# Moving four tile pools by 64 or 96 bytes in a float32 diffusion-transformer kernel

## The chip, the cores and the metric

The kernel runs on one core of one Trainium2 chip. The metric is the device time of one execution in microseconds (us), a median over runs. TensorE multiplies, with a stationary operand that is loaded first (a weight load, PEld in the profile) and a streamed operand that passes through it (the matmul, PE). VectorE (DVE), ScalarE (ACT) and GpSimd (POOL) do the elementwise work, SyncE (SP) starts most of the transfers.

## What is computed

Two layers of a diffusion transformer over 512 latent tokens and, in the first layer, 256 context tokens, model width 1024, all in float32. Both layers scale and shift their input with values made from a conditioning vector, and both end in a gated feed-forward block. Layer 0 mixes tokens by grouped attention (16 heads, 4 key heads, width 64, rotary embedding), layer 1 by a gated linear recurrence in two directions (8 heads of 128):

```python
for i in range(DEPTH):
    hn_l = modulate(rms_norm(h, norm_mix_w[i]), sh1_l, sc1_l)
    hn_c = modulate(rms_norm(hc, norm_mix_w[i]), sh1_c, sc1_c)
    y_l, y_c = attention_mixer(...) if i == 0 else hgrn2_mixer(...)
    h = h + gt1_l * y_l
    h = h + gt2_l * swiglu(modulate(rms_norm(h, norm_ffn_w[i]), sh2_l, sc2_l), ffn_w_in[i], ffn_w_out[i])
    if not last: hc = ...            # the same for the context
return rms_norm(h, final_norm_w)
```

## The kernel before

**Stages, in order of time.** To about 430 us: conditioning values, keys and values, queries, attention and its output projection. 430 to 940 us: the feed-forward block of layer 0 over 768 tokens, in two column blocks of 384. 940 to 1420 us: the recurrence, head by head. From 1420 us: the feed-forward block of layer 1 over 512 tokens, in two column blocks of 256, and the output.

**Products.** A product in float32 is made of two parts, high and low, of each operand, and of three matmuls (`mm3`, lines 116 to 120: high times high, high times low, low times high). Each matmul has a 128x128 stationary operand, which is loaded anew for every matmul, and streams 256, 384 or 512 columns. In both feed-forward blocks, the weights of a hidden tile are combined so that seven products of 12 matmuls do the work of eight (`pair_units`, line 1213; `m1` to `m7`, lines 1082 to 1130): they stream the operands `xb11`, `xb21`, `xt1`, `xt2`, `xt4`, `xb22` and `xt3` in this order (in layer 1, `xb11` and `xb21` lie in a tile called `xw`). The first hidden tiles are made plainly (`plain`, line 1039, tile `ffi`). The second half of the block streams the hidden values `gh` and `gl` and keeps the output weights stationary (`fo_mm`, line 1133, tile `ffo`). In the recurrence, `hz` and `hq` (`trans_proj`, line 1626) stream the normalised input `hn` over stationary weights, and `hv` and `hg` (`token_proj`, line 1615) stream the weights over stationary `hn`. In attention, `po` (line 798) streams the probabilities `pth` and `ptl` over the stationary values `vv`. The scan itself (`lv`, line 1725) streams `QD` over the stationary `kc`. `wo` and `hwo` stream attention's and the recurrence's result (`o`, `oth`) over stationary output weights.

**Where tiles lie.** A tile takes the same bytes in each of 128 partitions. The program rounds a tile up to 32 bytes and puts it behind the one before; pools are stacked from the low end, or from the high end (`side="right"`; within such a pool the first tile is still the lowest). So the byte address of each operand follows from the sizes. Weights on their way to TensorE lie in `ring`, whose tiles all start at a multiple of 128. The other operands start, modulo 128, at:

| operand (pool) | streamed or stationary | start mod 128 |
|---|---|---|
| `whi`, `wlo` (`ring`) | stationary, in `hv` and `hg` streamed | 0 |
| `hnh`, `hnl` of layer 0 (`hn0p`) | stationary | 96 |
| `pth`, `ptl` (`att`); `vv` | streamed; stationary | 0; 0 |
| `o` (`o4p`), `oth`, `otl` (`hgrno`) | streamed | 96 |
| `xb11`, `xb21`, `xt4`, `xb22`, `xt2` of layer 0, `hn` of layer 1 (`hnp`) | streamed, in `hv` and `hg` stationary | 0 |
| `xt3`, `xt1` of layer 0 (`ffn0`) | streamed | 0, 64 |
| `gh`, `gl` of layer 0 (`ffn0`, `ffn0g`) | streamed | 32 or 64, by the slot |
| `kc`, `QD` (`hgrn`) | stationary, streamed | 32, 32 |
| `xw`, `xt4`, `xb22`, `xt3` of layer 1 (`ffn1`) | streamed | 0 |
| `xt1`, `xt2` of layer 1 (`ffn1`) | streamed | 32, 64 |
| `gh`, `gl` of layer 1; `foh`, `fol` (`ffn1`) | streamed; stationary | 32 or 64; 64 |

The text calls the difference of the two starts modulo 128 the offset of a matmul. With weights in `ring` it is the start of the other operand. A tile that comes to lie on the bytes of older tiles waits for their last users.

**The three tiny tiles** hold reciprocal root mean squares, six numbers a partition (24 bytes, so 32). `rstd_of` (line 290) makes them; `rc0` and `rc1` are made in the feed-forward blocks (lines 1330, 1343 and 1427), the third in `norm_tail` (line 1565), in the pool `ffn0g`.

Of the kernel before, what the change touches and what calls it, by code (L numbers as in the profile page):

```python
# [8 lines left out]
F32 = mybir.dt.float32  # L9
# [7 lines left out]
P = 128  # L17
D = 1024
KT = D // P
NL = 512  # L20
NC = 256
T = NL + NC
NT = T // P
# [26 lines left out]
def kernel(  # L50
# [13 lines left out]
    def pool(name, es=None, **kw):  # L64
        return (es or ctx).enter_context(tc.tile_pool(name=name, bufs=1, reuse_waits="tile", **kw))
# [16 lines left out]
    def bank(name):  # L82
        return psums["pool"].tile([P, 512], F32, tag="b", bufs=psums["bufs"]["b"], name=name)
# [32 lines left out]
    def mm3(ps, ahi, alo, bhi, blo, first, last, onto=False):  # L116
        kw = dict(skip_group_check=True) if onto else {}
        PE.matmul(ps, ahi, bhi, start=first, stop=False, **kw)  # L118
        PE.matmul(ps, ahi, blo, start=False, stop=False, **kw)  # L119
        PE.matmul(ps, alo, bhi, start=False, stop=last, **kw)  # L120
# [160 lines left out]
    def rstd_cols(pl, acc, n, tag="rc", late=False):  # L281
        nt = n // P
        pc = bank("ssq")
        for t in range(nt):
            m = PE.matmul(pc[:, 2 * t : 2 * t + 2], acc[:, t * P : (t + 1) * P], ones[:, 0:2], start=True, stop=True)
            if late:
                pin(m)
        return rstd_of(pl, pc, nt, tag)

    def rstd_of(pl, pc, nt, tag="rc"):  # L290
        rc = pl.tile([P, NT], F32, tag=tag, name="rc")[:, :nt]
        DVE.tensor_scalar(rc, pc[:, 0 : 2 * nt].rearrange("p (t v) -> p t v", v=2)[:, :, 0], 1.0 / D, EPS,
                          op0=ALU.mult, op1=ALU.add)
        POOL.tensor_tensor(rc, rc, mhalf.to_broadcast([P, nt]), op=ALU.pow)
        return rc

    def rstd_psum(dg, rc, n, late=False):
        nt = n // P
        dg = dg[:, 0:n].rearrange("p (t q) -> p t q", q=P)
        DVE.tensor_tensor(dg, ident.unsqueeze(1).to_broadcast([P, nt, P]), rc.unsqueeze(2).to_broadcast([P, nt, P]),  # L300
                          op=ALU.mult)
        ps = bank("rstd")[:, 0:n]
        for t in range(nt):
            m = PE.matmul(ps[:, t * P : (t + 1) * P], ones, dg[:, t], start=True, stop=True)
            if late:
                pin(m)
        return ps
# [33 lines left out]
    hnp = pool("hn0p", qes, side="right")  # L341
# [399 lines left out]
    qes.close()  # L741

    hpool = pool("hT", side="right")
    hT = [hpool.tile([P, T], F32, name=f"hT{k}") for k in range(KT)]

    def residual_in():
# [12 lines left out]
    def residual(o, ps, layer, ch, v, a, e):  # L759
        DVE.scalar_tensor_tensor(hT[o][:, a:e], ps, mcol(layer, ch, o, v), hT[o][:, a:e], op0=ALU.mult, op1=ALU.add)  # L760

    ap_ = pool("att", att)
    o4es = ExitStack()
    o4p = pool("o4p", o4es, side="right")
    lasts = []
# [104 lines left out]
    acc_n = pool("accn").tile([P, T], F32, name="acc_n")  # L870
# [8 lines left out]
    def xbank(name):  # L879
        return xps["pool"].tile([P, 512], F32, tag="x", bufs=6, name=name)  # L880
# [3 lines left out]
    def wo_last():  # L884
        (ws, prs), = lasts
        for half in HALVES[0]:
            a0, e0 = half[0][1], half[-1][2]
            banks = {}

            def wos(o, i):  # L890
                if o not in banks:
                    banks[o] = xbank("wos")
                osl = slice(o * P, (o + 1) * P)
                mm3(banks[o][:, 0 : e0 - a0], ws[i][0][:, osl], ws[i][1][:, osl],
                    prs[i][0][:, a0:e0], prs[i][1][:, a0:e0], i == 0, i == 1)

            if a0 == 0:
                for o in range(4):
                    wos(o, 0)
            for o in range(KT):  # L900
                if o not in banks:
                    wos(o, 0)
                wos(o, 1)
                ps = banks.pop(o)
                for v, a, e in half:
                    residual(o, ps[:, a - a0 : e - a0], 0, 2, v, a, e)
                yield
        o4es.close()
# [38 lines left out]
    def ffn(layer, only_lat, pre, begin, tail=None):  # L947
# [4 lines left out]
        parts = PARTS[layer]  # L952
        es = ExitStack()
        fp = pool(f"ffn{layer}", es)

        def operand(m, slot=None):
            p_ = fp if layer or m in ("t1", "t3") else hnp
            if layer and m in ("b11", "b21"):
                if not wide_op:
                    wide_op.append(p_.tile([P, 4, 4, H], F32R, tag="xw", name="xw"))  # L960
                i = 2 * (m == "b21")
                return [wide_op[0][:, i], wide_op[0][:, i + 1]]
            return [p_.tile([P, 4, H], F32R, tag=f"x{slot or m}{c}", name=f"x{m}{c}") for c in "hl"]
# [353 lines left out]
        rc, rst = {}, {}  # L1317
# [244 lines left out]
    rst1 = [None, None]  # L1562
    hg = ExitStack()

    def norm_tail(fp, o):
        if o == 2:
            rst1.append(rstd_cols(fp, acc_n[:, :NL], NL))
        elif o == 4:
            rst1[0] = rstd_psum(fp.tile([P, T], F32, tag="g8", bufs=1, name="dg"), rst1.pop(), NL)

    hnp = pool("hnp", hg)
    ffn(0, False, wo_last(), ada_mix, tail=norm_tail)
    xps["es"].close()
    s2es = ctx.enter_context(ExitStack())
# [355 lines left out]
    for _ in sb:  # L1930
        pass
    hg.close()
    ffn(1, True, wlast, None)


# [46 lines left out]
```

## Time and profile before

| | |
|---|---|
| median of 3 runs | 1802.15 us (1801.05 to 1806.98) |
| the profiled execution | 1801.19 us, its span from first to last instruction 1799.4 us |
| busy: PE, PEld, DVE, ACT, POOL | 97%, 89%, 72%, 48%, 35% of the span |
| instructions | 30616, of which 11717 matmuls and as many weight loads |
| mean granted TensorE clock | 0.994 |

The profile gives for each engine the time in which it worked on something; a matmul's time is counted from its first column to its last result, and the next one starts long before that end. How fast TensorE goes is therefore read from the starts of successive matmuls in the timeline, not from the time of one. Groups of instructions are written as line, engine, operation, tile written and tiles read, stationary columns and streamed shape, count, busy us and mean ns of one, and the engine's idle time before them.

### The profile page before, as it was taken

What the parts mean: (1) busy time and instruction counts of PE and PEld (TensorE: products, weight loads), DVE (VectorE), ACT (ScalarE), POOL (GpSimd) and SP (SyncE); (2) the same over time, 40 slices, a digit from 0 to 9 for tenths busy, and PEclk for the clock granted to TensorE, in tenths of its full rate; (3) what the DMA queues carried; (4) which work ended last, traced back from release to release, by engine and by line L of the source; (5) the groups of instructions that cost most, each with busy time, mean ns of one, the idle gap of its engine ahead of it and who ended that gap; (6) DMA issues with size and microseconds to landing.
All of it is one profiled execution on the core that took longest, in us unless ns stands there. A gap on an engine that the chain in (4) does not pass through costs nothing.

```text
span 1799.4 us, 30616 instructions
## 1 busy us (share of the span) xinstructions
PE 1745.2 (97%) x11717; PEld 1601.1 (89%) x11717; DVE 1301.7 (72%) x2281; ACT 871.7 (48%) x1777; POOL 624.2 (35%) x570
## 2 busy tenths in 40 slices
PE   8999999999899999999999999999999899999998
PEld 6788788898899989999998999898898899999997
DVE  4876788888878888888866555655747658786764
ACT  3544777766533524243446433334334545554544
POOL 2454344434113314132303243224425454333420
PEclk9999999999999999999999999999999899999999
DMA  9534400002134242545331212123211124343322
GB/s 334 174 123 131 148 28 25 24 1 77 33 109 123 65 131 86 164 136 158 94 106 46 71 59 78 53 71 94 71 48 47 56 60 115 100 116 99 100 61 83
DMA packets 213457, 166.42 MB, mean 92 GB/s; under 512 B 7952, under 2 KB 190400, under 8 KB 213312
## 3 DMA queue, kind: packets, MB, share of 16 engines
q1 hardware_dynamic: 213024, 163.43, 29.8%
q8 instruction: 92, 1.51, 0.3%
q10 hardware_dynamic: 288, 1.05, 0.1%
q14 instruction: 53, 0.43, 0.1%
HBM read 162.36 MB, written 2.10 MB: 91 GB/s over the span
## 4 chain that ended last, share of the span: by engine, by line
PE 79%; DVE 8%; ACT 4%; issue 4%; POOL 3%; DMA 2%; SPq 0%; POOLq 0%; ACTq 0%; DVEq 0%
PE ffo L120 5%; PE ffo L118 5%; PE ffo L119 5%; PE x L118 4%; PE x L119 4%; PE x L120 4%; PE pt L787 3%; PE y L118 2%; PE lv L1725 2%; PE y L119 2%; PE y L120 2%; PE hz L118 2%; PE hz L119 2%; PE hz L120 2%; PE sc L729 1%
## 5 line engine op out<-in xcount | busy, mean ns | idle before, releaser
L1732 POOL TENSOR_TENSOR KD<-KD,tot 128x384 f32<-128x384 f32 x96 | 102.8, 1094 | 81.7 <-ACT kc L1715 77.9
L777 POOL TENSOR_SCALAR pf<-pf,st 128x768 f32<-128x768 f32 (+1 forms) x96 | 73.7, 769 | 125.7 <-DVE st L776 89.4
L760 DVE SCALAR_TENSOR_TENSOR hT<-ffo,modc,hT 128x512 f32<-128x512 f32 (+1 forms) x122 | 78.6, 648 | 45.0 <-PE ffo L120 45.0
L120 PE MATMUL ffo<-gh,wlo_w 128*128 128x512 f32 (+1 forms) x304 | 102.6, 338 | 0.0
L119 PE MATMUL ffo<-gl,whi_w 128*128 128x512 f32 (+1 forms) x304 | 102.2, 336 | 0.0
L118 PE MATMUL ffo<-gh,whi_w 128*128 128x512 f32 (+1 forms) x304 | 101.7, 337 | 0.0
L95 DVE TENSOR_TENSOR ptl<-pt,pth 128x384 fp32r<-128x384 f32 (+1 forms) x160 | 79.8, 523 | 12.8 <-ACT pth L90 11.6
L242 DVE SCALAR_TENSOR_TENSOR adacc<-adw,csil,adacc 128x512 f32<-128x512 f32 x98 | 83.3, 860 | 7.7 <-DMA adw<-in_ada_w_dram 7.6
L90 ACT CAST pth<-pt 128x384 fp32r<-128x384 f32 (+1 forms) x160 | 69.8, 461 | 34.0 <-PE pt L787 22.1
L775 ACT ACTIVATE pf<-sc,st 128x768 f32<-128x768 f32 (+1 forms) x96 | 73.5, 765 | 19.0 <-DVE st L773 18.0
L1732 DVE TENSOR_TENSOR QD<-QD,tot 128x256 f32<-128x256 f32 x96 | 52.0, 581 | 41.2 <-PE lv L1725 41.1
L773 DVE TENSOR_REDUCE st<-sc 128x1 f32<-128x768 f32 (+1 forms) x96 | 74.1, 773 | 10.2 <-PE sc L730 8.7
L1715 ACT COPY kc<-KD 128x256 f32<-128x256 f32 x112 | 43.3, 413 | 76.3 <-PE lv L1725 44.5
L787 PE MATMUL pt<-ident,pf 128*128 128x128 f32 x448 | 72.1, 275 | 5.2 <-DVE ptl L95 3.8
L118 PE MATMUL ffo<-gh,foh 128*128 128x512 f32 (+1 forms) x186 | 71.4, 384 | 0.0
L120 PE MATMUL ffo<-gh,fol 128*128 128x512 f32 (+1 forms) x186 | 70.8, 381 | 0.2 <-DVE fol L95 0.2
L119 PE MATMUL ffo<-gl,foh 128*128 128x512 f32 (+1 forms) x186 | 70.9, 381 | 0.0
L1791 POOL TENSOR_SCALAR oss<-oss 128x4 f32<-128x4 f32 (+1 forms) x9 | 4.7, 525 | 181.8 <-DVE oss L1790 181.7
L1725 PE MATMUL lv<-QD,kc 128*128 128x128 f32 x448 | 63.4, 286 | 4.5 <-DVE QD L1732 2.4
L1725 PEld LDWEIGHTS lv<-QD,kc 128*128 128x128 f32 x448 | 58.6, 191 | 8.8 <-ACT kc L1715 3.8
L787 PEld LDWEIGHTS pt<-ident,pf 128*128 128x128 f32 x448 | 51.3, 140 | 13.9 <-issue 6.4
L119 PEld LDWEIGHTS ffo<-gl,whi_w 128*128 128x128 f32 x304 | 57.2, 188 | 6.9
(1114 smaller groups left out, 6772.5 us busy)
## 6 DMA issues: line engine op xcount, KB each, us to landing
adw<-in_ada_w_dram SPq DMA_DIRECT2D x40, 512.0 KB, 4.6
adw<-in_ada_w_dram SPq DMA_DIRECT2D x80, 256.0 KB, 2.9
raw_hz<-in_hgrn_w_in_dram SPq DMA_DIRECT2D x14, 512.0 KB, 3.7
adr<-in_ada_w_dram SPq DMA_DIRECT2D x16, 256.0 KB, 5.4
adr<-in_ada_w_dram SPq DMA_DIRECT2D x8, 512.0 KB, 7.9
raw_wq<-in_attn_w_qkv_dram SPq DMA_DIRECT2D x8, 512.0 KB, 5.4
raw_wo<-in_attn_w_o_dram SPq DMA_DIRECT2D x8, 512.0 KB, 3.4
raw_hv<-in_hgrn_w_in_dram SPq DMA_DIRECT2D x8, 512.0 KB, 4.3
```

The source lines that it names most:

```text
L95: m = (eng or DVE).tensor_tensor(lo, src, hi.bitcast(F32), op=ALU.subtract)
L118: PE.matmul(ps, ahi, bhi, start=first, stop=False, **kw)
L119: PE.matmul(ps, ahi, blo, start=False, stop=False, **kw)
L120: PE.matmul(ps, alo, bhi, start=False, stop=last, **kw)
L242: pin(DVE.scalar_tensor_tensor(a, raw, cc, a, op0=ALU.mult, op1=ALU.add))
L760: DVE.scalar_tensor_tensor(hT[o][:, a:e], ps, mcol(layer, ch, o, v), hT[o][:, a:e], op0=ALU.mult, op1=ALU.add)
L773: DVE.tensor_reduce(st3[:, 0:1], ps[:, :nk], op=ALU.max, axis=AX.X, negate=True)
L775: ACT.activation(pf, ps[:, :nk], AF.Exp, bias=st3[:, 0:1], accum_out=st3[:, 1:2])
L777: POOL.tensor_scalar(pf, pf, st3[:, 2:3], 1.0, op0=ALU.mult, op1=ALU.mult)
L787: PE.transpose(pt[:, i * P : (i + 1) * P], pf[:, (i0 + i) * P : (i0 + i + 1) * P], ident)
L1725: PE.matmul(ps[:, cs], kc[:, cs], mv, start=True, stop=True)
L1732: eng.tensor_tensor(view, view, f, op=ALU.mult)
```

## The change

Four pools begin with a tile that nothing uses, and three tiny tiles get longer. No instruction is added or taken away.

```diff
     def rstd_of(pl, pc, nt, tag="rc"):
-        rc = pl.tile([P, NT], F32, tag=tag, name="rc")[:, :nt]
+        rc = pl.tile([P, {"rc0": 32, "rc1": 32, "rct": 16}.get(tag, NT)], F32, tag=tag, name="rc")[:, :nt]
...
     hpool = pool("hT", side="right")
+    hpool.tile([P, 24], F32, name="shift")
...
     ap_ = pool("att", att)
+    ap_.tile([P, 16], F32, name="shift")
...
         fp = pool(f"ffn{layer}", es)
+        if layer:
+            fp.tile([P, 16], F32, name="shift")
...
     def norm_tail(fp, o):
         if o == 2:
-            rst1.append(rstd_cols(fp, acc_n[:, :NL], NL))
+            rst1.append(rstd_cols(fp, acc_n[:, :NL], NL, "rct"))
...
     hnp = pool("hnp", hg)
+    hnp.tile([P, 16], F32, name="shift")
```

By the same rule of sizes, everything in `att` moves up by 64 bytes; everything in `hnp`, and in `hgrn` and `ffn0` which lie on top of it, by 64; everything in `ffn1` by 64; in `ffn0` and `ffn1`, what lies behind `rc0` by 96 more, and behind `rc1` by another 96. On the right side, `hT` stays, and `o4p` and `hgrno` below it move down by 96, `ffn0g` by 96 and 32. The starts become:

| operand | start mod 128 before | after |
|---|---|---|
| `pth`, `ptl` (over `vv` at 0) | 0 | 64 |
| `o`, `oth`, `otl` | 96 | 0 |
| `xb11`, `xb21`, `xt4`, `xb22`, `xt2`, `xt3` of layer 0; `hn` of layer 1 | 0 | 64 |
| `xt1` of layer 0 | 64 | 64 |
| `gh`, `gl` of layer 0 | 32 or 64 | 64 |
| `kc`, `QD` | 32, 32 | 96, 96 |
| `xw`, `xt4`, `xb22`, `xt3`, `xt1`, `xt2` of layer 1 | 0, 0, 0, 0, 32, 64 | 64 |
| `gh`, `gl` of layer 1 over `foh`, `fol` | 32 or 64 over 64 | 64 over 64 |

So matmuls with `ring` weights in the feed-forward blocks, `hz`, `hq`, `hv`, `hg` and `po` come to an offset of 64. `ffo` of layer 1, `wo` and `hwo` come to, or stay at, an offset of 0, and the scan's stay at 0.

## The prediction

> **What bounds the kernel now.** I read the page first, then the busy time by stage, then the timeline of TensorE matmul by matmul, then the groups by shape.
>
> ```profile
> PE 1745.2 (97%) x11717; PEld 1601.1 (89%) x11717; DVE 1301.7 (72%) x2281; ACT 871.7 (48%) x1777; POOL 624.2 (35%) x570
> ...
> PE 79%; DVE 8%; ACT 4%; issue 4%; POOL 3%; DMA 2%; SPq 0%; POOLq 0%; ACTq 0%; DVEq 0%
> ```
>
> TensorE is the bound: busy for 97% of the span, and 79% of the chain that ended last is its matmuls. The other engines can hardly become the bound through this change, which gives them no instruction.
>
> ```profile
> 430.00:940.00 510.00, 503.80 (x2877) 477.15 (x2876) 413.82 (x649) 211.71 (x418) 128.92 (x87) 1.00 0.36 107
> 940.00:1420.00 480.00, 469.88 (x3250) 432.05 (x3249) 295.11 (x491) 201.80 (x364) 166.97 (x154) 1.00 0.21 63
> 1420.00:1799.00 379.00, 364.00 (x2548) 340.38 (x2546) 266.55 (x443) 191.20 (x425) 143.25 (x110) 0.98 0.31 90
> ```
>
> The columns after the stage and its length are busy PE, PEld, DVE, ACT and POOL, then clock, transfers' share and GB/s. In the feed-forward block of layer 0 TensorE idles for 6 us of 510, in the recurrence for 10 of 480, at a full clock. In such stages a matmul that starts earlier moves everything behind it. So the question is whether the pace of the matmuls depends on where their operands lie. The same kernel already holds several offsets, in the same loop with the same weights tiles:
>
> ```profile
> 1506.39 0.28 PE L118 MATMUL x<-xt2h,whi_w 128*128 128x256 f32 x1
> ...
> 1507.81 0.28 PE L118 MATMUL w<-xt4h,whi_w 128*128 128x256 f32 x1
> ...
> 1581.44 0.28 PE L118 MATMUL x<-xt2h,whi_w 128*128 128x256 f32 x1
> ...
> 1582.80 0.28 PE L118 MATMUL w<-xt4h,whi_w 128*128 128x256 f32 x1
> ...
> 1601.22 0.28 PE L118 MATMUL x<-xt3h,whi_w 128*128 128x256 f32 x1
> ...
> 1602.66 0.28 PE L118 MATMUL x<-xw,whi_w 128*128 128x256 f32 x1
> ```
>
> Each pair of rows is the first matmul of a block of 12 and the first of the next block, all of 256 columns. The block with `xt3`, at offset 0, takes 1.44 us, so 120.0 ns from start to start. The blocks with `xt2`, at offset 64, take 1.42 us (118.3 ns) and, at 1581 us, 1.36 us (113.3 ns). Nobody waits in any of the three. So the offset seems to have a price for 256 columns, with two paces at 64. For longer streams:
>
> ```profile
> 530.20 0.39 PE L118 MATMUL ffo<-gh,whi_w 128*128 128x512 f32 x1
> ...
> 533.67 0.28 PE L118 MATMUL ffo<-gh,whi_w 128*128 128x256 f32 x1
> ...
> 580.27 0.33 PE L118 MATMUL y<-xt1h,whi_w 128*128 128x384 f32 x1
> ...
> 582.34 0.34 PE L118 MATMUL x<-xt2h,whi_w 128*128 128x384 f32 x1
> ...
> 584.45 0.33 PE L118 MATMUL w<-xt4h,whi_w 128*128 128x384 f32 x1
> ...
> 586.53 0.33 PE L118 MATMUL y<-xb22h,whi_w 128*128 128x384 f32 x1
> ...
> 1338.78 0.39 PE L118 MATMUL hz<-hnb11h,whi_hz 128*128 128x512 f32 x1
> ...
> 1344.22 0.60 PE L1810 MATMUL hot<-ident,on 128*128 128x128 f32 x4
> ...
> 1543.20 0.40 PE L118 MATMUL ffo<-gh,foh 128*128 128x512 f32 x1
> ...
> 1545.99 0.28 PE L118 MATMUL x<-xw,whi_w 128*128 128x256 f32 x1
> ```
>
> With 512 columns, the order is another one: 24 matmuls at offset 0 (`hz`) take 5.44 us, 226.7 ns each; 15 at offset 64 (`ffo` of layer 0) take 3.47 us, 231.3 ns each; 12 of which half are at offset 96 (`ffo` of layer 1) take 2.79 us, 232.5 ns each. With 384 columns, 12 at offset 64 (`xt1`) take 2.07 us and 12 at offset 0 (`xt4`) 2.08 us, 173 ns each; only the block between them, `xt2` at offset 0 behind `xt1` at 64, takes 2.11 us.
>
> **The change part by part.** The unused tiles and the longer ones issue nothing and hold nothing up by themselves; no wait is moved, no queue is passed. What could cost something is a moved tile that now touches one older tile more and waits for its last user. I went through the pools in order: nearly all tiles straddle two older ones already, since the tiles before them were of other sizes, and the few new edges (the first `x` tile over the tiny softmax tiles) are on tiles dead for long. I put this at 0. What remains is the pace of matmuls, in five terms, with counts from the loops.
>
> *1. 256 columns, offset 0 to 64.* In the feed-forward block of layer 1, five of the seven products of 12 matmuls, for 18 hidden tiles: 1080; its plain products: 240 (those with weights in `ring`). `hv` 4 x 6 x 24 = 576, `hg` 4 x 4 x 24 = 384, the context part of `hz` 384, and `po` 16 x 14 x 2 = 448. Together 3112. By the blocks above each gains from 1.7 to 6.7 ns.
>
> ```profile
> L118 PE MATMUL y<-xb22h,whi_w 128*128 128x256 f32 x72 | 20.4, 283 | 0.0
> ...
> L118 PE MATMUL x<-xt2h,whi_w 128*128 128x256 f32 x72 | 20.1, 279 | 0.0
> ```
>
> These groups of layer 1 differ by 4 ns in the mean time of one, which is not the pace but moves with it. I take 2.2 ns, near to the slow block, because the fast one follows a run at another offset and the change makes runs that begin as the slow one does, behind `ffo` at offset 0: 3112 x 2.2 = 6.8 us less. Ends: no gain, and 3112 x 6.7 = 20.9 us less.
>
> TensorE's rule in the Trainium skill speaks against this term: "TensorE: Matmul & The Clock Gate", section "Step-by-step: what each phase is for", says that the streamed operand and the weight load have independent read ports, so that loading the next weights takes nothing from the running matmul. By that the term would be 0; the trace disagrees by 1.7 ns a matmul or more, unless the order of the blocks makes it.
>
> *2. 512 columns, offset 0 to 64.* `hz` 336, `hq` 168 and the first head's 72: 576. The rows give a loss of 231.3 - 226.7 = 4.6 ns at most, since the `hz` run quoted is long and undisturbed; most others are cut by the scan's matmuls and are short. I take half: 576 x 2.3 = 1.3 us more. Ends: 0 and 2.6 us more.
>
> *3. 512 columns, offset 96 to 0.* `hwo` 144, `wo` 48, and `ffo` of layer 1 96: 288. From 232.5 ns to somewhere between 226.7 and 232.5; I take the middle, 2.9 ns less: 0.8 us less. Ends: 0 and 1.7 us less.
>
> *4. 384 columns.* Both offsets run at 173 ns; only the 0.03 us behind each switch from `xt1` to `xt2` goes, since both are at 64 afterwards: 20 hidden tiles, 0.6 us less. Ends: 0 and 0.6 us less.
>
> *5. 256 columns that come to offset 0* (the last `hwo`, part of `wo`, the plain products with weights in a moved slot): some 300 x 1.7 = 0.5 us more. Ends: 0 and 2.0 us (300 x 6.7) more.
>
> The scan's own matmuls keep their offset. The 448 transposes of the probabilities stream the identity over `pf`, which goes from 0 to 64 too; they run three at a time between other work, so I put them at 0, with 448 x 1.7 = 0.8 us less as the other end. The sum is -6.8 + 1.3 - 0.8 - 0.6 + 0.5 = -6.4 us of TensorE's time. In the feed-forward blocks all of it counts: 1320 x 2.2 = 2.9, 96 x 2.9 = 0.3 and 0.6, together 3.8 us. Of the other 2.6 us, which lie in attention and the recurrence, I let the chain's 79% count, 2.1 us; the rest would go into longer waits for ScalarE, VectorE and GpSimd, which are next there. That is 5.9 us less: 1801.19 - 5.9 = 1795.3 us in terms of the profiled execution, which is 1 us under the median of the runs shown (1802.15). About 0.3% (5.4 us) is what a measurement of this kernel can tell from no change.
>
> **Rivals.** *Nothing happens.* The paces belong to what ran before a block rather than to its operands, or the gains go into waits. For it: at 384 columns offsets 0 and 64 pace alike, and most of term 1 outside the feed-forward blocks sits beside other engines' work. Against it: `xt3` and `xt2` differ in every look at the same loop, and TensorE has no slack in the feed-forward blocks to lose it in. 1801.2 us.
>
> The section "Who interferes with whom" of the page "SBUF — State Buffer" in the Trainium skill stands for this one: it says that TensorE never waits for another reader. It speaks of other engines, so a conflict within TensorE would not contradict it; no row quoted here decides that.
>
> *The fast pace holds.* With whole runs of seven products at one offset, the pace of 113.3 ns could be kept from block to block. Then term 1 is 20.9 us: 1320 x 6.7 = 8.8, 0.9 as before, and 0.79 x (1792 x 6.7 = 12.0, less 1.3 and 0.5, plus 0.5) = 8.5, together 18.2 us less, 1783 us. For it: the block at 1581 us. Against: 12 matmuls later the next block has another offset, so nothing shows that it lasts, and the group's mean of 279 ns says that such blocks are few.
>
> *Slower: the switches.* The change puts runs at 64 next to runs at 0: `hz`, `hv` and `hg` between the scan's products (8 heads x 12 steps, 192 switches), `po` between score products (96), `ffo` of layer 1 between the seven products (64). If runs of 12 are too short to settle and each of these 350 switches costs the 0.03 us of the one before `xt2`, that is 10.5 us more against 6.4 less: 4.1 us, times 0.79 some 3 us more, 1804.4 us. It decides from 6.4 / 350 = 18 ns a switch on. Against: the switches with 256 columns in the quoted blocks show no such price, since 1.42 us includes the switch from `ffo` into `xt2`.
>
> **How the numbers follow.** My forecast has 0.60, nothing 0.20, the fast pace 0.12, the switches 0.08. The forecast's own range, from the takes of terms 1 to 3, is 1792 to 1799, and about two thirds of it lie beyond 0.3%: 0.39, with the fast pace 0.51 for faster. Slower by over 0.3% needs the switches at their full price and term 1 near zero: 0.06. The rest, 0.43, is the same. The range of 8 in 10, 1787 to 1803, takes in "nothing" and half of the way to the fast pace.
>
> **What would show it.** In the profile after: the same 30616 instructions; blocks with `xt3`, `xw`, `xb22` of layer 1 at 1.41 to 1.42 us for 12 instead of 1.44, `hv` likewise; the `xt2` block of layer 0 at 2.08 us; `hz` runs slower than 226.7 ns. Wrong would be: those blocks still at 1.44 us (the offset is not the cause), at 1.36 us (the fast pace holds), or right blocks with the span unchanged, when TensorE's idle time before the scan's and attention's matmuls must have grown.

## The result, and the profile after

| kernel | median | ratio to before, 95% interval |
|---|---|---|
| before, 6 runs | 1801.35 us (1800.63 to 1806.98) | |
| changed, 6 runs | 1793.57 us (1792.89 to 1797.23) | 0.9957 (0.9942 to 0.9973) |
| changed again, 5 later runs, before at 1803.46 beside them | 1793.90 us (1793.62 to 1798.92) | 0.9955 (0.9941 to 0.9968) |

The changed kernel is faster by 0.43%, some 7.8 us. The first page of the changed kernel, with the busy time by engine and the chain of waits, against the two lines quoted of before:

```profile
PE 1738.7 (97%) x11717; PEld 1594.5 (89%) x11717; DVE 1304.2 (73%) x2281; ACT 871.7 (49%) x1777; POOL 623.6 (35%) x570
...
PE 78%; DVE 8%; ACT 5%; issue 3%; POOL 3%; DMA 1%; SPq 0%; POOLq 0%; DVEq 0%; ACTq 0%
```

The same 11717 matmuls, 6.5 us less busy TensorE, the other engines within 2.5 us of before: the time comes from TensorE. The profiled execution was one of the longer ones (1796.98 us, span 1795.1). Its timeline shows where it lost part of the gain:

```profile
57.81 0.40 PE L120 MATMUL kv<-whi_wkv,hnl 128*128 128x512 f32 x1
```

The same matmul of before starts at 54.99 us, and no matmul ahead of it has got another difference of addresses, so I don't put these 2.8 us down to the change. I therefore read the stages from the second profile of the changed kernel, whose span is 1791.9 us. First the timeline of before, at the first matmuls of stages and 24 matmuls into the first `hv` run:

```profile
54.99 0.40 PE L120 MATMUL kv<-whi_wkv,hnl 128*128 128x512 f32 x1
...
440.71 0.42 PE L118 MATMUL ffi<-xb21h,whi_w 128*128 128x384 f32 x1
...
981.41 0.28 PE L118 MATMUL hv<-whi_hv,hnb11h 128*128 128x256 f32 x1
...
984.29 0.28 PE L118 MATMUL hv<-whi_hv,hnb11h 128*128 128x256 f32 x1
...
1442.44 0.36 PE L118 MATMUL ffi<-xw,w11h 128*128 128x256 f32 x1
```

And the same matmuls in the second profile of the changed kernel, with the blocks that the prediction named:

```profile
54.74 0.40 PE L120 MATMUL kv<-whi_wkv,hnl 128*128 128x512 f32 x1
...
440.11 0.42 PE L118 MATMUL ffi<-xb21h,whi_w 128*128 128x384 f32 x1
...
581.77 0.34 PE L118 MATMUL x<-xt2h,whi_w 128*128 128x384 f32 x1
...
583.85 0.34 PE L118 MATMUL w<-xt4h,whi_w 128*128 128x384 f32 x1
...
980.84 0.29 PE L118 MATMUL hv<-whi_hv,hnb11h 128*128 128x256 f32 x1
...
983.58 0.28 PE L118 MATMUL hv<-whi_hv,hnb11h 128*128 128x256 f32 x1
...
1334.07 0.39 PE L118 MATMUL hz<-hnb11h,whi_hz 128*128 128x512 f32 x1
...
1339.56 0.27 PE L1815 MATMUL hot<-ident,on 128*128 128x128 f32 x1
...
1438.33 0.36 PE L118 MATMUL ffi<-xw,w11h 128*128 128x256 f32 x1
...
1501.08 0.28 PE L118 MATMUL x<-xt2h,whi_w 128*128 128x256 f32 x1
...
1502.50 0.28 PE L118 MATMUL w<-xt4h,whi_w 128*128 128x256 f32 x1
...
1537.48 0.39 PE L118 MATMUL ffo<-gh,foh 128*128 128x512 f32 x1
...
1540.23 0.28 PE L118 MATMUL x<-xw,whi_w 128*128 128x256 f32 x1
...
1595.00 0.28 PE L118 MATMUL x<-xt3h,whi_w 128*128 128x256 f32 x1
...
1596.42 0.28 PE L118 MATMUL x<-xw,whi_w 128*128 128x256 f32 x1
```

The differences between these rows, and from the last one of a stage to the end of the span (1799.4 and 1791.9), give the stages:

| stage | before | changed | |
|---|---|---|---|
| start to keys and values | 54.99 | 54.74 | -0.25 |
| to layer 0's feed-forward block | 385.72 | 385.37 | -0.35 |
| to the first `hv` | 540.70 | 540.73 | +0.03 |
| recurrence | 461.03 | 457.49 | -3.54 |
| layer 1's feed-forward block, output | 356.96 | 353.57 | -3.39 |

The blocks show the paces, the time from the start of one matmul to the start of the next. The 24 matmuls of `hv` take 2.74 us instead of 2.88, 114.2 ns each instead of 120.0. The `xt3` block of layer 1 takes 1.42 us instead of 1.44, and the `xt2` block of layer 0 2.08 us instead of 2.11, both as said. 24 `hz` matmuls of 512 columns take 5.49 us (228.8 ns) instead of 5.44 (226.7): slower, as said.

### The profile page after: what moved, and what is told of

The parts are those of the page before. It is cut to its first block, busy times and chain, and to the rows that moved or that the text cites. A ratio compares the mean times of both kernels' runs of the same rounds, so it can differ in the third digit from the quotient of the medians.

```text
span 1795.1 us, 30616 instructions
## 1 busy us (share of the span) xinstructions
PE 1738.7 (97%) x11717; PEld 1594.5 (89%) x11717; DVE 1304.2 (73%) x2281; ACT 871.7 (49%) x1777; POOL 623.6 (35%) x570
## 4 chain that ended last, share of the span: by engine, by line
PE 78%; DVE 8%; ACT 5%; issue 3%; POOL 3%; DMA 1%; SPq 0%; POOLq 0%; DVEq 0%; ACTq 0%
PE ffo L118 5%; PE ffo L120 5%; PE ffo L119 5%; PE x L120 3%; PE x L119 3%; PE x L118 3%; PE lv L1730 3%; PE pt L789 3%; PE y L118 2%; PE y L119 2%; PE y L120 2%; PE hz L119 2%; PE hz L118 2%; PE hz L120 2%; PE sc L729 1%
## 5 line engine op out<-in xcount | busy, mean ns | idle before, releaser
L1796 POOL TENSOR_SCALAR oss<-oss 128x4 f32<-128x4 f32 (+1 forms) x9 | 4.7, 524 | 180.2 <-DVE oss L1795 180.1
L120 PEld LDWEIGHTS ffo<-gh,wlo_w 128*128 128x128 f32 x304 | 57.3, 188 | 6.6
```

## The experiments

The theory I began with: TensorE pays for the relation of the starts of streamed and stationary operand, modulo 128. Rivals: the absolute start of an operand counts; other engines' accesses collide with TensorE's; or only what ran before a block counts. "Difference" below is streamed start minus stationary start, and "64 over 0" is a streamed start of 64 over a stationary start of 0, by the bytes above a multiple of 128. A pace of "undisturbed" steps leaves out those with a wait in them.

**Addresses by themselves.** A kernel that only multiplies, in runs of 96; the three matmuls of each of its steps:

```python
PE.matmul(ps, wh[:, c], a, start=k == 0, stop=False)
PE.matmul(ps, wh[:, c], b, start=False, stop=False)
PE.matmul(ps, wl[:, c], a, start=False, stop=k == 3)
```

> This kernel leaves out all of the reference's work: it fills some tiles with one 128x1024 block of the input and then only multiplies, on TensorE alone, in runs of 96 matmuls (8 groups of 12, in the order high-high, high-low, low-high of the kernel) over one pair of start addresses each; the tiles' names tell the bytes above a multiple of 128 (m64x streamed, s0w stationary). No other engine reads or writes meanwhile. The theory that TensorE itself pays for the relation of the two starts expects, for 256 columns, 120.0 ns from start to start at difference 0, whatever the absolute place (0 over 0, 64 over 64 and 32 over 32 alike), and 113 to 118 ns at difference 64; for 512 columns 226.7 ns at 0 and 229 to 232 at 64; for 384 columns 173.3 at both. The rival that the absolute place counts expects 64 over 64 to pace like 64 over 0. The rival that other engines' accesses make the difference expects all differences to pace alike here, since there are none. The rival that only what ran before a run sets its pace expects the runs behind an idle gap to pace alike whatever their difference, and the runs without a gap to follow the run ahead of them.

Measured, for 256 columns: 64 over 0 at 117.7 ns behind a gap, and at 113.3 in five of six runs without one; 0 over 64 at 117.8; 0 over 0 at 118.6, 32 over 32 and 64 over 64 at 120.0; 4 bytes over 0 at 123.3. With no other engine at work the paces still differ by address, so other engines' accesses aren't needed. But several expectations failed. One difference has two stable paces, held over some 70 matmuls, by how the run begins. 0 over 0 was faster than 32 over 32 and 64 over 64. 384 columns ran at 176.0 ns at difference 0 and 176.6 at 64, not at 173.3. And 512 columns ran at 233 ns at difference 0 as well as at 64, not at the kernel's 226.7. My tiles in this kernel were an odd multiple of 128 bytes long, so that tiles with one name modulo 128 lay at two places modulo 256, which only the next runs brought out.

**The relation, or the place.** Two kernels with one edit, the ring of weights 64 bytes lower and all else in place:

```diff
-        a_c = cst.tile([P, KT, 2], F32, name=f"a_ffn{layer}")
+        a_c = (ring if layer else cst).tile([P, KT, 2], F32, name=f"a_ffn{layer}")
```

On the kernel before:

> The kernel before, with one edit: a tile of 64 bytes goes from the end of the constants to the end of the ring of weights, so that the ring's tiles begin 64 bytes lower and everything above them stays where it was. No streamed tile of the feed-forward blocks moves, but 2664 of the 3112 matmuls of 256 columns of term 1 (all but po) get the difference 64 that they have in the changed kernel; 502 others (xt2 of layer 1, parts of the second products) go from 64 to 0, and the 576 of 512 columns from 0 to 64 as in the change. The theory that the relation of the two starts counts expects nearly the change's gain: those 2664 are worth 9.0 of the 9.6 us that term 1 brought in the trace, 502 x 2 = 1 us goes back, so 6 to 8 us less than before, 1794 us. The rival that the absolute place of the streamed operands counts expects no change, 1801 us.

Measured 1798.35 us against 1802.06, ratio 0.9984 (0.9975 to 0.9993): faster, by less than half of what I expected. On the changed kernel:

> The changed kernel with the same edit on top: streamed operands of the feed-forward blocks and stationary ones of the recurrence stay at 64, as changed, but the ring begins at 64 too, so that the 2664 matmuls are at difference 0 again. Only po (448) keeps the change's difference. The relation theory expects the gain to be gone but for po's 0.6 us, 1800 to 1802 us. The rival that the absolute place counts expects 1793.6 us, as changed.

Measured 1809.27 us, ratio 1.0039 (1.0027 to 1.0052): slower than the kernel before, which neither theory expects. The timelines of the two: first the ring alone,

```profile
988.69 0.29 PE L118 MATMUL hv<-whi_hv,hnb11h 128*128 128x256 f32 x1
...
991.42 0.28 PE L118 MATMUL hv<-whi_hv,hnb11h 128*128 128x256 f32 x1
...
1601.72 0.28 PE L118 MATMUL x<-xt3h,whi_w 128*128 128x256 f32 x1
...
1603.13 0.28 PE L118 MATMUL x<-xw,whi_w 128*128 128x256 f32 x1
```

then both:

```profile
585.13 0.34 PE L118 MATMUL x<-xt2h,whi_w 128*128 128x384 f32 x1
...
587.24 0.34 PE L118 MATMUL w<-xt4h,whi_w 128*128 128x384 f32 x1
...
589.35 0.34 PE L118 MATMUL y<-xb22h,whi_w 128*128 128x384 f32 x1
...
988.40 0.28 PE L118 MATMUL hv<-whi_hv,hnb11h 128*128 128x256 f32 x1
...
991.28 0.28 PE L118 MATMUL hv<-whi_hv,hnb11h 128*128 128x256 f32 x1
...
1609.55 0.28 PE L118 MATMUL x<-xt3h,whi_w 128*128 128x256 f32 x1
...
1610.98 0.28 PE L118 MATMUL x<-xw,whi_w 128*128 128x256 f32 x1
```

For 256 columns the relation is what counts: with the ring moved, 24 `hv` matmuls take 2.73 us, though the stationary `hn` lies where it lay, and the `xt3` block of layer 1 1.41 us, though its streams lie where they lay; with both moved it is 2.88 and 1.43 us again. Summed over the kernel, `hv` saves 3.12 us with the ring alone and 3.07 us in the change. The surprise is in the longer streams. With both moved, blocks of 384 columns take 2.11 us for 12 (175.8 ns), where the difference is 0 modulo 128 as before; most ran at 173 ns before. `hq` (512 columns) goes from 232.9 ns in the mean to 236.5, the products `y` of layer 0 over `xb22` from 176.7 to 184.4. (These means have the waits in them.) The ring had moved down and the operands up, by 64 each: their difference was 128, not 0. With the ring alone, `xt1` of layer 0 and `xt2` of layer 1 got 128 in the same way. In its profile the recurrence takes 5.6 us less than before and layer 1's block 1.9, but the stretch from layer 0's block to `hv` 2.7 more (543.43 us); that is where a part of the expected gain may have gone. Another part is in attention: the ring also moved under `q` and `kv`, which the expectation leaves out (224 instead of 32 modulo 256); their matmuls take 1.9 us more, steps with a wait left out. Another 4.1 us of that one execution had been lost by the first row of `kv` (59.11 us), of which I can't say that the edit caused it.

**A part alone.** The shift of `ffn1` and the tiny tiles, without `hnp`, `att` and `hT`:

> Only the part of the change in layer 1's feed-forward block (its unused tile, and the longer tiny tiles): 1320 of the 3112 matmuls of 256 columns get difference 64 and its second products 0; attention, layer 0's block and the recurrence keep their old differences, but for layer 0's second products, whose streams go to 0. If the parts act by themselves and all of TensorE's saving counts in that block, 4.2 us less than before, as the trace after shows from the start of that block on: 1797 us. If a gain there were eaten by waits, less than 1 us. If the saving of the recurrence was needed for it (a state carried from one block to the next), 0 to 2 us.

Measured 1800.26 us, ratio 0.9986 (0.9977 to 0.9996). In its trace layer 1's block and output take 3.34 us less than before, as in the change (3.39), and the recurrence is within 0.2 us of before. So the parts act by themselves. The kernel as a whole gained some 2 us less than I expected; here, too, the stretch of layer 0's block is longer (by 1.9 us), with `gh` at differences that the full change does not have. How much of this 1.9 us and of the 2.7 us above is the edits' is not shown: six profiles of the change and of its variants below, with the same differences in that stretch, have it at 539.2 to 541.9 us. Layer 1's block is steadier: 353.4 to 353.7 us in this profile, the two of the change and that of the all-64 kernel below.

**Which modulus.** The second kernel of matmuls alone, with starts 128 to 1024 bytes further up:

> Again only matmuls of TensorE over tiles filled once, the reference's work left out; now in a fixed order, with finer differences, with streams 128 to 1024 bytes further up at the same difference modulo 128, with 256 columns behind runs of 512 or 128 columns, and with differences 112 and 124 for 384 and 512 columns. The theory that the start modulo 128 and the way a run begins set the pace expects 113.3 ns at 112 behind a gap and without one, as in the first such kernel, the same paces for starts further up, and at 64 either 113.3 or 117.7 ns, by the run ahead. The rival that larger address differences count expects the paces at 0 and 64 to change with the 128 to 1024 bytes. If only the run ahead counts, 0 and 64 behind the same 24 matmuls of 512 columns pace alike.

Measured for 256 columns: at name 112, 117.1 ns, but 113.3 when 128 further up, and 117.1 again at 256, 512 and 1024 further up; at name 0, 118.6 ns, 120.0 at 128 further up, 118.6 at the others (though the same place held 120.0 in one of its two runs behind a gap); at name 64, 117.8 ns at all five. So at 112 the 128 bytes change the pace and 256 don't: the difference counts modulo 256, not modulo 128. (In this kernel, name 112 is a difference of 240, and 112 is reached 128 further up; name 64 is 64, where in the first kernel it was 192.) Behind 24 matmuls of 512 columns, 0 ran at 118.6 to 120.0, 64 at 117.8 and name 112 at 117.1 ns, so the run ahead does not decide alone. Three kernels put this to the test in layer 1's first seven products; the first two are equal to the change modulo 128, the third has 112 there:

```diff
-        rc = pl.tile([P, {"rc0": 32, "rc1": 32, "rct": 16}.get(tag, NT)], F32, tag=tag, name="rc")[:, :nt]
+        rc = pl.tile([P, {"rc0": 32, "rc1": 32, "rct": 16}.get(tag, NT) * (1 + (nt == 2 and tag != "rc"))], F32, tag=tag, name="rc")[:, :nt]
```

> The changed kernel; the two tiny tiles of layer 1's block are 256 bytes instead of 128, so that there all streamed operands of the first seven products stand 64 above the ring's weights modulo 256 (in the changed kernel xt1 stands at 192, the others at 64), and all second products at 0 modulo 256 instead of some at 128. Modulo 128 nothing moves. The theory that the differences count modulo 128 expects no change against the changed kernel, 1793.6 us. The theory that they count modulo 256, as the kernel with the ring and the changed operands both at 64 suggests (its difference is 128 there: 384 columns at 176 ns, 512 at 233 ns), expects 96 second products of 512 columns to go from 232 to 228 ns, 0.4 us less. If the switch to xt1 and back is what ends the 113.3 ns in which that block begins, the products behind it keep 113.3 ns for a part of the hidden tiles, 1 to 4 us less.

With `fp.tile([P, 48], F32, name="shift")` instead of 16 words on top of that:

> As the one before, and layer 1's block begins 128 bytes higher: its streamed operands all stand 192 above the ring's weights instead of 64. Modulo 128 again nothing moves, so the theory of differences modulo 128 expects 1793.6 us. The theory modulo 256 takes 192 as the difference of hv and hg in the changed kernel (ring streamed, operands stationary), which run at 114.2 ns where the products of layer 1 at 64 run at 117.5: 1296 x 3.3 = 4.3 us less than the changed kernel, 1789 us. If the way a run begins decides and not the difference, the two kernels with 64 and 192 are equal.

With slices 48 bytes into longer tiles, so that the streams begin at 112:

```diff
-                    wide_op.append(p_.tile([P, 4, 4, H], F32R, tag="xw", name="xw"))
+                    xw = p_.tile([P, 16 * H + 64], F32R, tag="xw", name="xw")
+                    wide_op.append(xw[:, 12 : 12 + 16 * H].rearrange("p (a k n) -> p a k n", a=4, k=4))
...
+            if layer:
+                ts = [p_.tile([P, 4 * H + 64], F32R, tag=f"x{slot or m}{c}", name=f"x{m}{c}") for c in "hl"]
+                return [t[:, 12 : 12 + 4 * H].rearrange("p (k n) -> p k n", k=4) for t in ts]
...
```

> As the first of these, but the streamed operands of the first seven products of layer 1 are slices that begin 112 bytes above a multiple of 256, and the weights that lie in their tiles begin at a multiple of 256, so that these 1512 matmuls stand 112 apart (144 of them at 0 or 128 before). The kernel of TensorE alone gave 113.3 ns at a difference of 112 modulo 256 behind a gap and without one, and 117.1 at 240, which is the same modulo 128. The theory modulo 256 expects 113.3 ns in all seven products: 1296 x 4.2 = 5.4 us and 144 x 6.5 = 0.9 us less than the changed kernel, 1787 us. The theory modulo 128 has 112 as 240 and expects 117.1 ns, 0.5 us less. If 113.3 needs the history of that kernel, no change.

and the changed kernel beside them:

> The changed kernel itself beside the other three on one chip, so that they can be compared with it and not only with the kernel before: 0.9957 of before, as measured at first, if chips agree; 0.994 to 0.997 by the interval there.

| difference in layer 1's first seven products | median | ratio to before |
|---|---|---|
| 64, `xt1` at 192 (the change) | 1793.90 | 0.9955 (0.9941 to 0.9968) |
| all 64 | 1793.84 | 0.9941 (0.9927 to 0.9954) |
| all 192 | 1795.07 | 0.9955 (0.9942 to 0.9967) |
| all 112 | 1788.26 | 0.9913 (0.9900 to 0.9927) |

The all-64 kernel can't be told from the change, and its products `x`, `y`, `z`, `w` run at 117.0 to 118.3 ns, as they did (117.1 to 118.6): removing the switch to `xt1` and back didn't keep 113.3, so that idea falls. All 192 brought nothing either, against what I expected from `hv`:

```profile
1596.43 0.28 PE L118 MATMUL x<-xt3h,whi_w 128*128 128x256 f32 x1
...
1597.85 0.28 PE L118 MATMUL x<-xw,whi_w 128*128 128x256 f32 x1
```

1.42 us, as at 64; and `ffi`, which ran at 113.5 ns at 64, runs at 118 here. At 112:

```profile
1592.64 0.28 PE L118 MATMUL x<-xt3h,whi_w 128*128 128x256 f32 x1
...
1594.01 0.28 PE L118 MATMUL x<-xw,whi_w 128*128 128x256 f32 x1
```

1.37 us, 114.2 ns each; over the groups of the seven products the undisturbed steps take 113.4 to 114.7 ns. Layer 1's block and output take 348.5 us (1438.19 to 1786.7) instead of 353.6. This version is 5.6 us faster than the change and 0.87% faster than the kernel before.

It would be faster still, but the second products slowed down, at a difference that did not move. All 498 `ffo` matmuls of 512 columns stand at 0 modulo 256 in the all-64 kernel and in this one, and their undisturbed steps take 228.5 ns there and 231.4 here, 1.4 us in all. A run of 15, first in the all-64 kernel,

```profile
1613.40 0.40 PE L118 MATMUL ffo<-gh,foh 128*128 128x512 f32 x1
...
1616.81 0.28 PE L118 MATMUL x<-xw,whi_w 128*128 128x256 f32 x1
```

then in the kernel with 112:

```profile
1607.01 0.40 PE L118 MATMUL ffo<-gh,foh 128*128 128x512 f32 x1
...
1610.48 0.28 PE L118 MATMUL x<-xw,whi_w 128*128 128x256 f32 x1
```

The steps of the first run come down to 226 to 227 ns after two matmuls, those of the second after eleven: 3.41 and 3.47 us. So a run has to settle, and how long that takes depends on the run ahead of it.

**The map.** A last kernel of matmuls alone, with all starts placed modulo 256:

> Again only matmuls of TensorE over tiles filled once, the reference's work left out: 48 matmuls at each of the 16 differences that are multiples of 16 bytes modulo 256 (the names of the tiles tell it), for 256, 384 and 512 columns, once behind an idle gap and once behind 12 matmuls of 512 columns at difference 0. The theory modulo 256 expects for 256 columns 113.3 ns at 112 both times, 117.1 at 240, 117.7 at 64 and 117.7 or 113.3 at 192, 118.6 at 128, 120.0 or 118.6 at 0; for 384 columns 173.3 at 0 and 64, 176 at 128; for 512 columns 226.7 to 228 at 0, 229.3 at 64, 233 at 128 and 192. The theory modulo 128 expects each difference to pace like the one 128 further up. Differences with the pace of 16 cycles over the columns at 384 and 512 (166.7 and 220 ns) aren't expected by either; if there are some, layer 0's block could gain up to 12 us.

Rows of its timeline, the 13th and the 37th matmul of a run, at 112, 192 and 240 behind a gap, then at 112 and 192 behind matmuls of 512 columns:

```profile
71.53 0.28 PE L115 MATMUL bk1z<-m112x,s0w 128*128 128x256 f32 x1
...
74.25 0.28 PE L115 MATMUL bk1z<-m112x,s0w 128*128 128x256 f32 x1
...
103.66 0.28 PE L115 MATMUL bk1z<-m192x,s0w 128*128 128x256 f32 x1
...
106.38 0.28 PE L115 MATMUL bk1z<-m192x,s0w 128*128 128x256 f32 x1
...
123.24 0.28 PE L115 MATMUL bk1z<-m240x,s0w 128*128 128x256 f32 x1
...
126.04 0.28 PE L115 MATMUL bk1z<-m240x,s0w 128*128 128x256 f32 x1
...
190.79 0.28 PE L115 MATMUL bk1z<-m112x,s0w 128*128 128x256 f32 x1
...
193.51 0.28 PE L115 MATMUL bk1z<-m112x,s0w 128*128 128x256 f32 x1
...
232.76 0.28 PE L115 MATMUL bk0z<-m192x,s0w 128*128 128x256 f32 x1
...
235.58 0.28 PE L115 MATMUL bk0z<-m192x,s0w 128*128 128x256 f32 x1
```

24 matmuls take 2.72 us at 112 both times (113.3 ns) and 2.80 at 240 (116.7 by these two rows; 117.1 over 35 of them). At 192 it is 2.72 us behind the gap and 2.82 us (117.5) behind the others. Mean paces of the last 35 in ns, for six of the 16 differences, behind a gap / behind 512 columns where they differ:

| difference mod 256 | 256 columns | 384 | 512 |
|---|---|---|---|
| 0 | 120.0 (behind 512 columns; the other run was the kernel's first, at 157) | 173.3 | 226.7 |
| 64 | 117.8 | 173.3 | 228.9 |
| 112 | 113.3 | 173.3 / 173.4 | 231.1 / 231.3 |
| 128 | 118.7 / 119.9 | 175.6 | 232.4 / 233.5 |
| 192 | 113.3 / 117.8 | 173.3 / 176.7 | 233.4 / 233.3 |
| 240 | 117.1 | 180.1 | 233.3 |

Of differences that are equal modulo 128, 112 and 240 pace differently at every length, 0 and 128 at 384 and 512 columns. None of the 16 ran below 173.3 ns at 384 columns or below 226.7 at 512, so the first seven products of layer 0 have nothing to gain in this way. Two kernels more, on the one with 112. First its block 128 bytes higher (48 words instead of 16 in the unused tile):

> The kernel with differences of 112 in layer 1's block, begun 128 bytes higher: the same 1512 + 240 streams by the ring's weights now stand 240 above them modulo 256, which is the same modulo 128 (the 144 by weights in the block's own tiles keep 112). The theory modulo 128 expects the time of the kernel with 112, 1788.3 us. The theory modulo 256 takes 117.1 ns at 240 from the kernel of TensorE alone, where 112 gave 113.3: 1752 x 3.5 = 6.1 us more, 1794 us.

Measured 1792.94 us, ratio 0.9948 (0.9935 to 0.9960). The block of its timeline,

```profile
1594.34 0.28 PE L118 MATMUL x<-xt3h,whi_w 128*128 128x256 f32 x1
...
1595.74 0.28 PE L118 MATMUL x<-xw,whi_w 128*128 128x256 f32 x1
```

takes 1.40 us, 116.7 ns, and layer 1's block with the output 352.5 us (1437.91 to 1790.4) instead of 348.5. The same places modulo 128, another pace, and 4.7 us more in the median than the next kernel, which keeps 112 in this block and ran beside it: this settles the modulus in the kernel itself. Second, `o`, `oth` and `otl` from 128 to 0:

```diff
-    hpool.tile([P, 24], F32, name="shift")
+    hpool.tile([P, 56], F32, name="shift")
...
-{"rc0": 32, "rc1": 32, "rct": 16}
+{"rc0": 32, "rc1": 32, "rct": 48}
```

> The kernel with differences of 112, and the unused tile ahead of hT 224 bytes instead of 96, with the one tiny tile of layer 0's norm 128 bytes longer so that its second products stay where they are. Attention's last heads and the recurrence's outputs (192 matmuls of 512 columns, 96 of 384, 144 of 256) go from difference 128 modulo 256 to 0; modulo 128 they stay at 0. The theory modulo 256 expects 192 x 5 + 96 x 2.5 - 144 x 1.2 = 1.0 us less TensorE time, by the map's 232.4 to 226.7, 175.6 to 173.3 and 118.7 to 120.0 ns, of which some 0.6 to 0.8 us counts: 1787.6 us beside 1788.3. The theory modulo 128 expects 1788.3 us. By this little the times alone can't decide; the pace of hwo and wo in the trace can.

Measured 1788.28 us, ratio 0.9922 (0.9909 to 0.9935): not to be told from the kernel with 112 (0.9913, measured on another chip). The undisturbed steps of `hwo` with 512 columns went from 232.4 to 231.4 ns (`oth`) and from 231.7 to 229.3 (`otl`), those of `wo` over `o` from 232.8 to 230.2, a fifth to a half of the 5.7 ns that the map gives; their runs are short and begin behind others.

## Why the prediction was right, point by point

**The forecast and its mechanism.** 1795.3 us was forecast, 1793.57 measured. The step on which it rests, that the start of the streams against the weights sets the pace, held; the moved ring shows it in layer 1's block without moving a stream. The Trainium skill's rule, weighed there against it, from "TensorE: Matmul & The Clock Gate", "Step-by-step: what each phase is for" (independent read ports, so nothing to gain), does not agree with the 113.3 and 117.1 ns at 112 and 240 that TensorE shows with every other engine idle.

**Term 1** was 9.6 us of TensorE time, not 6.8 (from start to start, both traces matched matmul by matmul): `hv` 3.07, `ffi` 1.46, `hg` 1.29, `x` 0.96, `hz` 0.76, `po` 0.68, `z` 0.51, `y` 0.45, `w` 0.32, `h` 0.10. The take of 2.2 ns from the slow `xt2` block was right for `x`, `y`, `z` and `hz` (2.1 to 2.4 ns), and a little high for `w` and `po` (1.5). It was wrong for `hv` (5.3), `hg` (3.4) and `ffi` (6.1): 1200 of the 3112 settled at 113 to 115 ns. The step that failed there is that "the change makes runs that begin as the slow one does": the products behind `ffo` do, these three do not. `ffi` stands at 64 like those products; `hv` and `hg`, in which the weights are streamed, stand at 192 modulo 256. So the rival of the fast pace holds in two places, and not in the one for which I weighed it. That this came out near the forecast is in part luck: the modulus was wrong, but all matmuls of this term came to 64 or 192, all but `po`'s from 0, and none to 128.

**Term 2** was 0.4 us, not 1.3: the map has 228.9 ns at 64, not the 231.3 from which I took half. The prediction reads the 15 `ffo` matmuls of that 231.3 as all at 64; by the sizes of the tiles six stood at 192, four at 64 and five at 32 modulo 256. **Term 3** was about 0, not -0.8: `ffo` -0.13, `wo` and `hwo` +0.6 with their waits and 0.04 without. They came to 128 modulo 256, where 512 columns take 232 ns as they did at 224. Here, and in the price of term 2, the wrong modulus of the prediction cost it something. **Term 4** was -0.78 (predicted -0.6), **term 5** +0.2 (+0.5). The prediction left out the second products of layer 0, whose `gh` moved too; they came to -0.2 us.

**What passes to the end.** Layer 1's block gained 3.39 us, about what its matmuls saved: 3.7 by the terms above and 0.5 of all its `ffo` with 512 columns (0.4 of it in the 402 that kept their difference), less term 5 and 0.64 us that `xt2` lost. Three of the 18 `xt2` blocks ran at 113.3 ns before, and some 0.4 us of the loss is a longer wait in the first block. The recurrence gained 3.54 us of the 4.2 that I count there (`hv`, `hg`, `hz`, less `hz` and `hq` with 512 columns and `hwo`), 84% where 79% was put; but five other profiles with the same differences there have it 2.9 to 5.3 us shorter than before, so this share is not measured so closely. Layer 0's block lost its 0.78 us again: one wait of the first `x` over `xt2` for ScalarE, at 790 us, grew from 0.23 to 0.90 us. The waits put at 0 were thus some 1.1 us in these two profiles. Together -7.5 us in the clean profile, against -5.9 predicted; nearly all of the difference is term 1.

**The slower rival** had switches at 30 ns each. That they cost little follows from the sum and was not measured apart: term 1 came out above its take although all those switches were there. What makes such a change slower is another mechanism, not on my list: a difference of 128 under 384 and 512 columns, some 7 us in the kernel with both moved.

## What to carry to other kernels

When TensorE is the bound and every matmul loads new weights, take the start-to-start pace of undisturbed runs from the timeline, group it by length and by streamed start minus stationary start modulo 256, and place the tiles for the lengths that fill the time: here 112 for 256 columns, 0 for 512, 0 or 64 for 384. An address experiment must control more bits than its theory names. Price a pace by the runs that it will really have, since at one difference two paces can hold, and look at the runs behind the ones that moved: they can lose a part of the gain, as `ffo` did.

## What the runs showed of the hardware that was not expected

At each length the lowest pace and a second one lie 6.7 ns apart: 113.3 and 120.0 ns at 256 columns, 173.3 and 180.1 at 384, 226.7 and 233.3 at 512. Most others lie between (117.8 ns at 64 is a repeating mix of steps of 117, 118 and 119), a few above. At difference 192, 256 columns hold 113.3 or 117.8 ns over whole runs, and `hv`, `hg` (114 to 116) and layer 1's products (117.8) take one each in one kernel or the next. At 64 the same holds for `ffi` (113.5) and the products behind `ffo` (117.5), and the 48 matmuls of 256 columns of the recurrence's first head ran at 113.3 in the all-64 and all-192 kernels and at 117.8 in the change, with the same differences. 512 columns at 240 ran at 236.7 ns in the second kernel of matmuls and at 233.3 in the third. What decides at the start of a run is open: a gap led to 117.7 in the first kernel of matmuls and to 113.3 in the third. Why 112 settles at the fast pace is open as well; the runs show that it does, behind a gap, behind 512 columns and in all seven products. Starts that are not multiples of 16 were tried only between 100 and 124 and at 4 and 8, where none was faster than 119.4 ns.
